# Weight low parts made by an accumulating transfer instead of a VectorE subtraction

## The chip, the cores and the metric

The kernel runs on one core of a Trainium2 chip as a single launch. The time is device microseconds from the first to the last instruction of that core with what the launch adds around it; lower is better. Before the change it is 884.13 us (median of 3 runs, 882.3 to 887.68).

## The reference

Two small transformer stacks stand one behind the other, in fp32, on 256 tokens of width 1024. The first has two layers (a sliding-window attention with sinks, then a block attention), the second two layers that each hold a hybrid mixer (dilated attention beside a state-space model) and a SwiGLU feed-forward of hidden width 2816. Cut to what matters here:

```python
for i in range(2):                                  # first stack
    q, k, v, z = split_proj(rmsnorm(h, norm_g[i]), w_in[i], n_kv)
    h = h + (attention(q, k, v) * silu(z)) @ w_out[i]
for l in range(2):                                  # second stack
    h = h + hybrid_mixer(rmsnorm(h), w_in_2[l], ..., w_out_2[l])
    y = rmsnorm(h)
    h = h + (silu(y @ w_gate[l]) * (y @ w_up[l])) @ w_down[l]
return rmsnorm(h)
```

Nearly all of the arithmetic is `x @ w` with weights that are used once: 141 MB of them are read from memory in each execution. The products have to be close to fp32.

## The kernel before, in words

**Split products.** TensorE multiplies in a rounded fp32 format (`F32R`). Each operand is therefore split into a rounded high part and the low part that is left over, `lo = raw - hi`, and each product is three: hi by hi, hi by lo, lo by hi. For the weights the split is done in `feed`: a raw tile lands from memory (`raw`, up to 8 rows of 128x256), and for each pair of its rows (128x512 elements, 256 KB) a `hi` is cast from it on ScalarE, or on VectorE when VectorE is the earlier one by the planner's reckoning, and a `lo` is made by one VectorE subtraction (line 406). The two are pages of one pool of 64 pages that the activations share.

**Stages.** The stages are named a and ao (first layer and its output product), b and bo, m0, mo0, f0, fo0 (mixer, its output, gate and up products, down product of layer 0), then m1, mo1, f1, fo1. In the profile digits are left out, so `f` is both f0 and f1. A name's stage is the one that was being multiplied when the tile was made, so `f__lo` can hold weights of the down product that follows.

**Order.** A planner writes every engine's program before anything runs. `run_plan` keeps a reckoned clock for each engine (`clk`), issues the weight products of a fixed list slot by slot (one slot is 128 rows of K for 256 output columns), and lets the chains of attention, norms and gates take turns whenever their inputs are reckoned to be ready. `feed` issues casts ahead of the multiplication, `cast_slot` slots against `slot`, as far as pages and the reckoned lead of VectorE and ScalarE allow. Once written, each engine works through its list in order and waits on semaphores: an instruction that waits holds back all that stands behind it on its engine.

**Queues.** All weights are loaded on SyncE's queue in pieces of up to 1 MB into three raw buffers (`RAW = 3`); a load is issued when a buffer's casts are done. GpSimd computes 12 small powers for the norms (`columns`, `final`) and clears 12 small borders (`conv_unit`), and issues no transfers.

Line 78 is the helper that records every operation, so nearly all instructions of the profile stand under L78; the tiles' names tell them apart.

Of the kernel before, what the change touches and what calls it, by code (L numbers as in the profile page):

```python
# [11 lines left out]
F32 = mybir.dt.float32  # L12
F32R = mybir.dt.float32r
BF16 = mybir.dt.bfloat16
I32 = mybir.dt.int32
AF = mybir.ActivationFunctionType
OP = mybir.AluOpType
# [47 lines left out]
class Engine:  # L65


    def __init__(self, build, name, real):
        self.build, self.ename, self.real = build, name, real
# [43 lines left out]
class Build:  # L113
# [33 lines left out]
    SWAP = 100.0  # L147
    WARM = 13
    CAPS_AB = 6
    CAPS = {'mm': 5, 'sc': 3, 'tr': 2, 'pv': 2, 'out': 4}  # L150

    def __init__(self, ctx, tc, io):
        self.tc = tc
        self.nc = Engines(self, tc.nc)
        self.clk = dict(PE=0.0, DVE=0.0, ACT=0.0, POOL=0.0)
        self.cur = Chain(None, 0.0)
        self.cur.start = 0.0
        self.count = 0
        self.io = io
        self.n = 0  # L160
        self.phase = "i"

        def pool(name, bufs, **kw):
            return ctx.enter_context(tc.tile_pool(name=name, bufs=bufs, **kw))

        self.cp = pool("const", 1)
        self.wraw = pool("wraw", self.RAW)
        self.fp = pool("f", self.PAGES)
        self.xp = pool("x", 4)
        self.up = pool("u", 2)  # L170
        self.hp = pool("h", 6)
        self.sp = pool("s", 8)
        psum = dict(space=bass.MemoryType.PSUM)
        self.pp = pool("psum", 8, **psum)
        self.banks = [0.0] * 8
        self.used = dict(mm=0, sc=0, tr=0, pv=0, out=0)
        self.sides = []
        self.ups = self.raws = 0
        self.planned = {}
        self.landing = 0.0  # L180
        self.live = self.wlive = self.most = 0
        self.kept = {}
        self.x = Timed(self)
        self.res = Timed(self)
        self.plan = []
        self.dma_i = self.cast_i = self.cast_k = self.cast_slot = 0
        self.seg_i = self.seg_k = self.seg_m = self.slot = 0
        self.dma_at = 1200.0
        self.queue = self.nc.sync
        self.units = {}  # L190
        self.bubbles = {}


    def name(self, s):
# [89 lines left out]
    def bank_at(self, kind, n=1):  # L284

        if n > 1:
            if self.used[kind] + n > self.CAPS_AB or len(self.banks) < n:
                return None
            return sorted(self.banks)[n - 1]
        if self.used[kind] >= self.CAPS[kind] or not self.banks:  # L290
            return None
# [80 lines left out]
    def feed(self):  # L372

        nc = self.nc
        while self.dma_i < len(self.plan) and self.raws < self.RAW:
            self.feed_dma()
        while self.cast_i < self.dma_i and self.cast_slot < self.slot + self.LEAD:
            now = self.clk["PE"]
            urgent = self.cast_slot < self.slot + self.URGENT
            if not urgent and max(self.clk["DVE"], self.clk["ACT"]) > now + self.AHEAD:  # L380
                return
            s = self.plan[self.cast_i]
            if s["at"] > now:
                self.landing = s["at"]
                return
            k = s["k0"] + self.cast_k
            n = min(2, s["k1"] - k)
            if self.wlive >= self.WMIN and self.wlive + self.live + self.SPARE > self.PAGES:
                return
            self.wlive += 2  # L390
            raw = s["raw"][:, self.cast_k:self.cast_k + n, :]
            hi = self.fp.tile([P, n, S], F32R, tag="f", name=self.name("hi"))
            if s["mode"] == "dt":

                both = hi[:, :, 0:32]
                raw, hi, lo = raw[:, :, 0:16], both[:, :, 0:16], both[:, :, 16:32]
            else:
                lo = self.fp.tile([P, n, S], F32R, tag="f", name=self.name("lo"))
            at = s["at"]
            self.cur = Chain(None, at)  # L400
            self.cur.start = at
            if self.clk["DVE"] + self.SWAP < self.clk["ACT"]:
                nc.vector.tensor_copy(hi, raw)
            else:
                nc.scalar.activation(hi, raw, AF.Copy)
            nc.vector.tensor_sub(lo, raw, hi.bitcast(F32))
            for i in range(n):
                s["parts"][k + i] = ((both if s["mode"] == "dt" else hi)[:, i, :], lo[:, i, :], self.cur.ready)
            self.cast_k += n
            self.cast_slot += n  # L410
            if s["k0"] + self.cast_k == s["k1"]:
                self.cast_i += 1
                self.cast_k = 0
                if s["page"]:
                    self.drop()
                else:
                    self.raws -= 1

    def slot_ready(self):

        s = self.plan[self.seg_i]
        k = s["k0"] + self.seg_k
        if (s["xkey"], k) not in self.x or k not in s.get("parts", ()):
            return None
        t = max(self.x.at[s["xkey"], k], s["parts"][k][2])
        if s["first"] and self.seg_k == 0 and self.seg_m == 0:
            b = self.bank_at("mm", 2 if s["mode"] == "AB" else 1)
            if b is None or (s["mode"] == "half" and len(self.banks) < 2):
                return None
            t = max(t, b, sorted(self.banks)[s["mode"] == "half"])  # L430
        return t
# [1303 lines left out]
```

## Time and profile before

| | us |
|---|---|
| median of 3 runs | 884.13 |
| profiled execution | 884.43 |
| its span, first to last instruction | 882.4 |
| TensorE (PE) busy | 867.1 (98%) |
| VectorE (DVE) busy | 743.5 (84%) |
| ScalarE (ACT) busy | 546.7 (62%) |
| GpSimd (POOL) busy | 13.4 (2%) |
| DMA engines, share of 16 engines' span | 46.7% for 142.30 MB |

The first column of a stage in the profile's tables is its stretch of the span. A matmul's end is modelled and matmuls overlap in the pipeline, so the sum of their durations is more than the busy time; the busy time is their union. A group of instructions reads: engine, operation, out<-in by the tiles' names, partitions x elements, count, then busy time in all, mean ns of one, and the idle time ahead of them with what ended it.

### The profile page before, as it was taken

The page shows a single profiled execution, that of the slowest core. Times are in us where ns is not written, and L with a number is a line of the kernel's source. Part 1 is how long each engine was busy: PE and PEld are TensorE (multiplying, and loading weights), DVE is VectorE, ACT ScalarE, POOL GpSimd, SP SyncE. Part 2 cuts the span into 40 slices and gives each one's busy share as a digit, 9 for nine tenths or more (in the row PEclk, how much of TensorE's full clock was granted, in tenths as well). Part 3 has the DMA queues.
Part 4 walks back from the last instruction along what each step waited for, and adds up shares of the span by engine and source line. Part 5 has one row for each costly group of instructions (what it writes and reads, how often), then busy time and mean ns, then how long its engine had stood idle before and what let it go on. Part 6 is the DMA issues. An engine that isn't in the chain of part 4 may idle for free.

```text
span 882.4 us, 16918 instructions
## 1 busy us (share of the span) xinstructions
PE 867.1 (98%) x6451; PEld 795.9 (90%) x6451; DVE 743.5 (84%) x1677; ACT 546.7 (62%) x1289; POOL 13.4 (2%) x30
## 2 busy tenths in 40 slices
PE   8999999999999999999999999999999999999996
PEld 7987999879998899888888889999999888889996
DVE  5999899998999997999989478988978999888331
ACT  5468764788678775677556355677756676555321
POOL 0000000000100000000000000000000000000000
PEclk9999999999999999999999999999999999999998
DMA  8522675216620047767545537510247576535401
GB/s 301 196 97 73 232 270 173 94 59 220 230 97 13 14 144 233 267 208 269 197 175 167 204 123 289 189 49 2 60 156 263 196 263 209 191 132 190 157 1 48
DMA packets 30385, 142.30 MB, mean 161 GB/s; under 512 B 5344, under 2 KB 6880, under 8 KB 18400
## 3 DMA queue, kind: packets, MB, share of 16 engines
q1 hardware_dynamic: 30016, 141.08, 46.1%
q8 instruction: 51, 0.84, 0.4%
q14 instruction: 30, 0.25, 0.1%
q10 hardware_dynamic: 288, 0.14, 0.1%
HBM read 140.15 MB, written 1.05 MB: 160 GB/s over the span
## 4 chain that ended last, share of the span: by engine, by line
PE 63%; issue 22%; DVE 8%; DMA 4%; ACT 3%; SPq 0%; POOL 0%; POOLq 0%; DVEq 0%; ACTq 0%
PE m__p L78 20%; PE f__p L78 13%; PE b__p L78 8%; PE fo__p L78 7%; PE a__p L78 5%; PE mo__p L78 4%; PE bo__p L78 4%; PE ao__p L78 3%; DVE mo__lo L78 1%; DMA mo__raw<-wg 1%; DMA fo__raw<-wa 1%; DMA cst<-cst 1%; DVE f__lo L78 1%; DVE m__xs L78 1%; DVE m__lo L78 1%
## 5 line engine op out<-in xcount | busy, mean ns | idle before, releaser
L78 PE MATMUL f__p<-mo__x,f__hi 128*128 128x512 f32 x468 | 165.7, 395 | 0.0
L78 PE MATMUL f__p<-mo__x,f__lo 128*128 128x256 f32 x468 | 131.2, 280 | 0.0
L78 DVE TENSOR_TENSOR f__lo<-f__raw,f__hi 128x512 fp32r<-128x512 f32 x172 | 114.6, 688 | 3.8 <-ACT f__hi L78 1.9
L78 PEld LDWEIGHTS f__p<-mo__x,f__hi 128*128 128x128 f32 x468 | 87.7, 187 | 20.6
L78 ACT ACTIVATE f__hi<-f__raw 128x512 fp32r<-128x512 f32 x162 | 92.5, 622 | 0.1
L78 PEld LDWEIGHTS f__p<-mo__x,f__lo 128*128 128x128 f32 x468 | 88.4, 189 | 0.0
L78 PE MATMUL fo__p<-f__r,fo__hi 128*128 128x256 f32 (+1 forms) x300 | 71.3, 320 | 0.0
L78 PE MATMUL f__p<-f__x,f__hi 128*128 128x512 f32 x164 | 59.3, 395 | 0.0
L78 ACT ACTIVATE f__sum<-f__p 128x256 f32<-128x256 f32 x84 | 29.5, 383 | 44.6 <-PE f__p L78 44.6
L78 PE MATMUL fo__p<-f__r,fo__lo 128*128 128x256 f32 x200 | 56.3, 281 | 0.0
L78 PEld LDWEIGHTS fo__p<-f__r,fo__hi 128*128 128x128 f32 x300 | 49.9, 190 | 4.1
L78 PE MATMUL a__p<-fo__x,a__hi 128*128 128x256 f32 x272 | 51.5, 289 | 0.6 <-DVE fo__x L78 0.6
L78 DVE TENSOR_TENSOR fo__lo<-fo__raw,fo__hi 128x512 fp32r<-128x512 f32 (+1 forms) x58 | 36.1, 670 | 14.2 <-ACT fo__hi L78 11.7
L78 PE MATMUL mo__p<-mo__r,mo__hi 128*128 128x256 f32 x256 | 46.8, 284 | 1.1 <-DVE mo__r L78 1.1
L78 DVE TENSOR_TENSOR m__lo<-m__raw,m__hi 128x512 fp32r<-128x512 f32 x61 | 41.2, 686 | 6.9 <-ACT m__hi L78 6.5
L78 PE MATMUL f__p<-f__x,f__lo 128*128 128x256 f32 x164 | 46.0, 280 | 0.0
L78 PEld LDWEIGHTS a__p<-fo__x,a__hi 128*128 128x128 f32 x272 | 42.5, 192 | 2.5 <-issue 1.7
L78 PE MATMUL m__p<-bo__x,m__hi 128*128 128x256 f32 x232 | 44.3, 289 | 0.0
L78 ACT ACTIVATE mo__hi<-mo__raw 128x512 fp32r<-128x512 f32 x48 | 28.5, 626 | 24.3 <-DMA mo__raw<-wo 14.8
L78 DVE TENSOR_TENSOR mo__lo<-mo__raw,mo__hi 128x512 fp32r<-128x512 f32 x50 | 33.1, 688 | 12.3 <-ACT mo__hi L78 12.1
L78 ACT ACTIVATE fo__hi<-fo__raw 128x512 fp32r<-128x512 f32 (+2 forms) x59 | 30.8, 579 | 20.1 <-DMA fo__raw<-w 10.2
L78 PE MATMUL fo__p<-f__r,f__hi 128*128 128x256 f32 (+1 forms) x180 | 42.7, 319 | 0.0
(532 smaller groups left out, 2577.4 us busy)
## 6 DMA issues: line engine op xcount, KB each, us to landing
f__raw<-wu SPq DMA_DIRECT2D x18, 1024.0 KB, 4.9
f__raw<-wg SPq DMA_DIRECT2D x17, 1024.0 KB, 4.8
m__raw<-w SPq DMA_DIRECT2D x13, 1024.0 KB, 5.0
f__raw<-wd SPq DMA_DIRECT2D x10, 1024.0 KB, 4.9
b__raw<-wb SPq DMA_DIRECT2D x6, 1024.0 KB, 4.8
mo__raw<-wo SPq DMA_DIRECT2D x12, 512.0 KB, 4.2
fo__raw<-wd SPq DMA_DIRECT2D x6, 1024.0 KB, 4.9
fo__raw<-w SPq DMA_DIRECT2D x5, 1024.0 KB, 5.6
```

What stands on the lines that cost most here:

```text
L78: return fn(*args, **kw)
```

## The change

For a pair of rows that meets the conditions of `by_dma`, the low part is made in two steps: ScalarE writes the negated high part into `lo` (a copy with scale -1, rounded as `hi` is), and GpSimd issues a transfer that adds the same 256 KB of weights from memory onto it, so that `lo = -hi + raw`. Otherwise the subtraction on VectorE stays. The conditions: a full pair of an ordinary weight tile, cast at least 12 slots ahead of its use, GpSimd's reckoned clock not over 1 us past TensorE's, and ScalarE's reckoned clock earlier than VectorE's. The planner reckons 1300 ns of GpSimd and a further 3500 ns until the transfer has landed.

```diff
+    DMA_POOL = 1300.0
+    DMA_LAND = 3500.0
+    DMA_LEAD = 12
+    DMA_GAP = 0.0
+    NO_DMA = ()
...
-            nc.vector.tensor_sub(lo, raw, hi.bitcast(F32))
+            if self.by_dma(s, n):
+
+                nc.scalar.activation(lo, raw, AF.Copy, scale=-1.0)
+                self.tc.nc.gpsimd.dma_start(out=lo, in_=s["w"][s["unit"], :, k:k + n, :].bitcast(F32R), accum_op=OP.add)
+                self.clk["POOL"] = max(self.clk["POOL"], self.cur.ready) + self.DMA_POOL
+                self.cur.ready = self.clk["POOL"] + self.DMA_LAND
+                self.share[1] += 1
+            else:
+                nc.vector.tensor_sub(lo, raw, hi.bitcast(F32))
+                self.share[0] += 1
...
+    def by_dma(self, s, n):
+
+        return (s["mode"] in ("T", "AB", "tok") and not s["page"] and n == 2 and s["phase"] not in self.NO_DMA
+                and self.cast_slot >= self.slot + self.DMA_LEAD and self.clk["POOL"] < self.clk["PE"] + 1000.0
+                and self.clk["ACT"] + self.DMA_GAP < self.clk["DVE"])
```

Counted over the built programs: 277 low parts of 526 that VectorE subtracted go this way. By the weights they read, 20 belong to b, 52 to m0 and m1, 32 to the output products ao to mo1, 123 to f0 and f1 (60 and 63) and 50 to fo0 and fo1 (28 and 22); a has none. VectorE has 276 tensor_tensor fewer and, since it is now the earlier engine more often, 100 casts of high parts more (34 before, 134 after; 69 of the 100 are f's and fo's). ScalarE has 165 instructions more, which is 277 more less 112 that left it. The number of matmuls is the same, as is the number of transfers on SyncE's queue (196).

GpSimd's queue at the start of f0, where the norm's power stands (`f__s`), before the change:

```order
L78 TENSOR_TENSOR mo__s_4822<-mo__s_4820,mhalf 128x2
L78 TENSOR_TENSOR mo__s_4954<-mo__s_4952,mhalf 128x2
L78 TENSOR_TENSOR f__s_5412<-f__s_5410,mhalf 128x2
L78 TENSOR_TENSOR m__s_7506<-m__s_7504,mhalf 128x2
L78 MEMSET m__u_7589 128x2x3
```

and with it:

```order
L415 DMA f__lo_5469<-wg 128x512
L415 DMA f__lo_5501<-wu 128x512
L415 DMA f__lo_5506<-wu 128x512
L78 TENSOR_TENSOR f__s_5540<-f__s_5538,mhalf 128x2
L415 DMA f__lo_5553<-wg 128x512
L415 DMA f__lo_5578<-wu 128x512
L415 DMA f__lo_5605<-wu 128x512
```

The power that the norm of f0 needs now stands behind the transfers that were issued ahead of it, each of which waits for ScalarE's negated part.

ScalarE in the middle of f0 (`f__sum` reads a finished product, `f__gt` is the gate's tanh, `f__r` the split of the product's input for the next stage), before:

```order
L78 ACTIVATE f__hi_6177<-f__raw_6032 128x512
L78 ACTIVATE f__hi_6192<-f__raw_6077 128x512
L78 ACTIVATE f__r_6196<-f__sum_6143 128x256
L78 ACTIVATE f__r_6197<-f__sum_6143 128x256
L78 ACTIVATE f__sum_6208<-f__p_6137 128x256
L78 ACTIVATE f__sum_6208<-f__p_6138 128x256
L78 ACTIVATE f__hi_6225<-f__raw_6077 128x512
L78 ACTIVATE f__gt_6229<-f__sum_6208 128x512
```

and with the change:

```order
L78 ACTIVATE f__hi_6017<-f__raw_5865 128x512
L78 ACTIVATE f__lo_6018<-f__raw_5865 128x512
L78 ACTIVATE f__r_6027<-f__sum_5993 128x256
L78 ACTIVATE f__r_6028<-f__sum_5993 128x256
L78 ACTIVATE f__hi_6041<-f__raw_5865 128x512
L78 ACTIVATE f__lo_6042<-f__raw_5865 128x512
L78 ACTIVATE f__lo_6051<-f__raw_5865 128x512
L78 ACTIVATE f__sum_6061<-f__p_5987 128x256
L78 ACTIVATE f__sum_6061<-f__p_5988 128x256
```

Between two readings of finished products ScalarE now does up to five weight instructions where it did one or two.

VectorE in the same stage with the change (before, a subtraction `f__lo` stood at nearly every place between the others):

```order
L78 TENSOR_TENSOR f__sum_5807<-f__sum_5807,f__rowh_5594 128x512
L78 SCALAR_TENSOR_TENSOR f__gt_5820<-f__gt_5820,f__sum_5807 128x512
L78 CAST f__hi_5854<-f__raw_5662 128x512
L78 CAST f__hi_5874<-f__raw_5719 128x512
L78 TENSOR_TENSOR f__lo_5875<-f__raw_5719,f__hi_5874 128x512
L78 TENSOR_TENSOR f__sum_5867<-f__p_5799,f__sum_5867 128x256
L78 TENSOR_TENSOR f__sum_5867<-f__p_5800,f__sum_5867 128x256
```

Of the eight subtractions that two units need, about two are left in this stage, and casts have moved in.

## Rows read from the trace of the kernel before

**Rows 1.** The page: busy time and share of the span by engine, instructions.

```profile
PE 867.1 (98%) x6451; PEld 795.9 (90%) x6451; DVE 743.5 (84%) x1677; ACT 546.7 (62%) x1289; POOL 13.4 (2%) x30
```

**Rows 2.** Windows: stretch, length; busy by engine, PEclk, DMA share, GB/s.

```profile
0.00:50.00 50.00, 46.46 (x345) 43.61 (x346) 39.32 (x88) 26.09 (x60) 1.03 (x7) 1.00 0.67 241
50.00:100.00 50.00, 49.22 (x405) 41.93 (x404) 45.87 (x160) 38.25 (x117) 0.00 (x0) 1.00 0.29 99
100.00:850.00 750.00, 746.88 (x5502) 686.25 (x5502) 653.66 (x1422) 478.37 (x1106) 11.72 (x22) 1.00 0.48 166
850.00:882.40 32.40, 24.54 (x205) 24.07 (x203) 4.65 (x9) 4.02 (x8) 0.69 (x1) 0.89 0.10 33
```

**Rows 3.** Windows of 20 us around the idle places of the middle, same columns.

```profile
360.00:380.00 20.00, 19.38 (x113) 16.78 (x112) 19.45 (x39) 13.80 (x31) 0.69 (x1) 1.00 0.64 225
660.00:680.00 20.00, 18.90 (x159) 18.70 (x158) 16.51 (x31) 11.81 (x22) 1.07 (x1) 1.00 0.77 273
680.00:700.00 20.00, 19.01 (x113) 16.33 (x113) 19.46 (x40) 14.23 (x30) 1.07 (x1) 1.00 0.57 203
```

**Rows 4.** The chain that ended last, in f0: start us, us, what.

```profile
361.95 116.45 PE f__p L78 x672
```

**Rows 5.** Groups by form: the weights' splits on DVE and ACT.

```profile
L78 DVE TENSOR_TENSOR f__lo<-f__raw,f__hi 128x512 fp32r<-128x512 f32 x172 | 114.6, 688 | 3.8 <-ACT f__hi L78 1.9 <-DVE f__hi L78 0.5
L78 ACT ACTIVATE f__hi<-f__raw 128x512 fp32r<-128x512 f32 x162 | 92.5, 622 | 0.1
L78 DVE CAST f__hi<-f__raw 128x512 fp32r<-128x512 f32 x10 | 4.2, 422 | 0.0
```

**Rows 6.** Windows of the feed-forward stages: loads to last use, of f0, f0+fo0, f1, f1+fo1.

```profile
341.00:478.00 137.00, 136.38 (x822) 121.39 (x821) 126.49 (x240) 85.97 (x185) 0.69 (x1) 1.00 0.62 215
341.00:539.00 198.00, 197.38 (x1174) 175.18 (x1173) 165.34 (x316) 115.53 (x245) 0.69 (x1) 1.00 0.60 210
663.00:810.00 147.00, 144.91 (x872) 127.66 (x872) 132.42 (x242) 88.52 (x181) 1.07 (x1) 1.00 0.59 207
663.00:858.00 195.00, 192.91 (x1273) 175.66 (x1273) 153.50 (x276) 106.17 (x214) 1.07 (x1) 1.00 0.51 181
```

**Rows 7.** Window in which loads queue up, same columns.

```profile
16.00:22.00 6.00, 5.77 (x47) 5.55 (x47) 4.86 (x12) 4.06 (x12) 0.00 (x0) 1.00 1.01 409
```

**Rows 8.** The page: what the DMA engines moved over the span.

```profile
DMA packets 30385, 142.30 MB, mean 161 GB/s; under 512 B 5344, under 2 KB 6880, under 8 KB 18400
```

**Rows 9.** DMA issues: count, KB each, median us from issue to landing.

```profile
f__raw<-wg SPq DMA_DIRECT2D x17, 1024.0 KB, 4.8
...
mo__raw<-wo SPq DMA_DIRECT2D x8, 256.0 KB, 2.7
```

**Rows 10.** Instructions on one tile: ns min/median/max, first and last start us.

```profile
L1523 SPq DMA_DIRECT2D f__raw<-wg x17: 327/328/328, 357.3 to 754.8; - x17
...
L78 DVE TENSOR_TENSOR fo__lo<-f__raw,fo__hi x20: 683/686/693, 477.5 to 815.7; 128x512 fp32r<-128x512 f32 x20
...
L78 PE MATMUL fo__p<-f__r,fo__lo x200: 279/280/283, 500.7 to 872.0; 128*128 128x256 f32 x100
```

**Rows 11.** GpSimd's groups: the norms' powers.

```profile
L78 POOL TENSOR_TENSOR m__s<-m__s,mhalf 128x2 f32<-128x2 f32 x4 | 4.9, 1223 | 323.6 <-DVE m__s L78 322.8 <-ACT m__dT L78 0.7
L78 POOL TENSOR_TENSOR f__s<-f__s,mhalf 128x2 f32<-128x2 f32 x2 | 1.8, 878 | 64.3 <-DVE f__s L78 64.3
```

More of the change, by code (lines that the diff above doesn't have):

```diff
@@ L191, in __init__ @@
         self.bubbles = {}
+        self.share = [0, 0]
     def name(self, s):
```

## Prediction, before the changed kernel ran

> **What bounds the kernel now.** I read the page's busy shares first, then the busy time by stretch, then the chain of waits, then the DMA shares of the stages that take most transfers.
>
> TensorE is busy for 867.1 of 882.4 us [rows 1]; VectorE, which the change relieves, for 743.5. A high share alone says little, since it is an average, so look at where TensorE is idle [rows 2]: 3.54 us in the first 50 us, 0.78 in the next 50, 7.86 after 850, and 3.12 us in the 750 us between. The start and the end have no transferred low part (a has none, and after 850 only the last products and the final norm are left). So TensorE's idle time that a faster VectorE could remove is those 3.12 us, and 2.7 of them stand in three places, the entries of f0 and f1 and the end of mo1: 0.62, 1.10 and 0.99 us [rows 3]. There the chain runs over VectorE and ScalarE. In the middle of f0 VectorE is at 92% (126.49 of 137 us) [rows 6] and yet the chain is one piece of 116.45 us of TensorE's own matmuls [rows 4]: VectorE is full but never late, and emptying it buys nothing there. The granted clock is 1.00 in all of it [rows 2], which is the upper level, 2.4 GHz.
>
> **The change part by part.**
>
> *VectorE.* A subtraction costs 114.6/172 = 0.666 us, a cast 4.2/10 = 0.42 us [rows 5]. 276 tensor_tensor fewer are -184 us, 100 casts more are +42: busy time falls from 743.5 to about 602 us. This lies beside TensorE's work except at the three places above.
>
> *ScalarE.* A cast of 128x512 costs 92.5/162 = 0.571 us [rows 5], and I take the same for the negated copy. 277 more and 112 fewer are about +94 us: 547 to 641, or 73%. In f0, where 88 of the low parts are cast (60 gate and up, 28 down, some of them after 478), it has 85.97 us of 137 [rows 6]; with all 88 there and no cast given away it would be 86 + 50 = 136 us, and with the 35 casts a layer that VectorE takes over (half of f's and fo's 69), about 116. Fuller than now, and less so than VectorE was without being late. ScalarE reads the finished products, though, so up to five weight instructions (2.9 us) can stand ahead of such a reading; a unit takes TensorE about 5.5 us (116.45 us for 672 matmuls at 32 a unit [rows 4]), and three units' products fit in the banks, so I cost that at nothing. If that cover went, each unit could be late by the 2.9 us.
>
> *GpSimd.* It issues 277 transfers. No row shows it issuing one. From below, SyncE takes 0.33 us to issue [rows 10]; from above I take the dearest thing that GpSimd does here, a norm's power at 1.22 us [rows 11]. In f0 the 60 gate and up transfers would take 20 to 73 us of 137. The powers now stand behind transfers: one that waits is late by one to two issues, 0.3 to 2.4 us. Only the powers at the entries of b, f0, m1 and f1 are followed at once by work that TensorE's next products end in, so the bounds are 0 and 4 x 2.4 = 10 us; I take 1 us, near the lower end, since products that need no row yet run on after the norm starts (TensorE lost just 0.62 us at the entry of f0 [rows 3]).
>
> *Landing.* A plain 256 KB load lands 2.7 us after its issue [rows 9]. A low part has far longer: the first subtraction for the down product starts at 477.5 and the first matmul with such a tile at 500.7 [rows 10], a lead of 23 us. Even three times the plain landing is hidden.
>
> *The DMA engines.* This is the term that decides. 277 x 0.262 MB are 72.6 MB on top of 142.3 [rows 8]. When loads queue up the engines move 409 GB/s at a share of 1.01 [rows 7]; over the stages they move 215 GB/s at 0.62 [rows 6], or 347 GB/s per full share. A plain 256 KB transfer is therefore 0.65 to 0.76 us of all 16 engines. What the addition costs, no row shows. The lower bound is that price; for an upper one I take two to three times it, since the engines must read the tile in SBUF as well as the weights, and write the sum.
>
> In f0 and fo0, from the first load (341) to the last down product (539), the weights themselves are 34.6 MB, 85 us at 409 GB/s or, by the share, 0.60 x 198 = 119 us with the next mixer's first loads in it [rows 6]. The 88 accumulating transfers add 57 to 67 us at the plain price: 142 to 186 of 198 us. So they fit, and the same holds for f1 and fo1 (0.51 x 195 = 99 us, and 85 transfers, 55 to 65 us: 154 to 164 of 195) [rows 6]. At twice the price the first is 199 to 253 of 198 and the second 195 to 229 of 195.
>
> **Sum.** The profiled execution took 884.43 us, 0.30 above the median of the three runs. From it I take 3.1 us of idle time that goes with VectorE's load, add 1 for the powers, and set the rest at nothing because TensorE covers it: 882.3. Matmuls' ends are modelled, so a pause that is shorter than a matmul's tail is not shown as idle; in the same three places some 1 to 2 us of that kind may go too. I forecast **881 us**. The bounds of this case alone: 884.4 - 6 = 878 (twice the shown idle time) and 884.4 + 7 = 891 (the powers late at their upper bound, 10 us, against 3 gained), and a few us lower than 878 if more pauses are hidden than I believe.
>
> **Rivals.**
>
> *The DMA engines become the bound in the feed-forward stages.* For it: f0 and f1 hold 123 of the 277, while 0.6 of the engines' time is already taken there [rows 6]. Against it: the average over the span is 47%, and the low parts have a 23 us lead. It decides from the point where the transfers do not fit: (198 - 119)/88 = 0.90 us of engine time each by the share, (198 - 85)/88 = 1.28 us by the saturated rate [rows 6, 7]. At 1.3 to 1.5 us each the excess is 1 to 55 us in layer 0 and 0 to 34 in layer 1, so the time is 881 plus some 0 to 89; half of it, 30 to 40 us, is not hidden by the lead, and I put this case at 890 to 925, most likely 907. Three times the plain price, 2 to 2.3 us, is 119 + 88 x 2.1 = 304 of 198 and 99 + 178 = 277 of 195, an excess of 188 us and a time near 1040. The sign of it would be TensorE waiting for `lo` or ScalarE for `raw` inside f0, where today it waits for nothing. This is the case on the other side. The Trainium skill, page "Collectives: The Full Stack", section "The bandwidth ceiling: the fold count and why AG ≠ RS ≠ AR", says that an addition in the transfer engines reads two sources through the same read ring, and gives 1.93 for the ratio measured there between plain and adding transfers. By that ratio an accumulating transfer here would be 1.25 to 1.47 us, the case just priced; no run here shows it yet.
>
> *GpSimd becomes the bound.* The 60 transfers of f0 leave 137/60 = 2.3 us each [rows 6]; from there on, low parts are late whatever the engines do. Twice the power's time, 2.4 us, would be just there; at 3 us the excess is 60 x 3 - 137 = 43 us a layer, of which the 23 us of lead take half: about 881 + 40 = 921. Nothing in the trace speaks for an issue that long.
>
> *VectorE's load is worth more than its idle places show.* If the attention stages have hidden pauses throughout, 9 to 12 us could go, 872 to 875. Against it: their idle time is nil, and the matmuls are the same in number and form.
>
> *The change doesn't do what it says* (too few transfers) is excluded by the count: 277 of 526.
>
> **How the numbers follow.** My forecast, no contention felt, has 0.47; the DMA bound at about twice the price 0.30, the dearer kinds of it 0.09, GpSimd's 0.06; VectorE's load worth more than shown 0.08. I call 1%, 8.8 us, the least that can be told from no change. The forecast case lies within 1%, and 0.03 of the DMA case at its mildest: 0.50. Faster by over 1% is the last of these cases, 0.08. Slower is the rest, 0.42. The range reaches from 873, in the middle of the fast case, to 922, which takes in most of the mild DMA case and GpSimd's at its mildest; the dearer ones, 0.09, and the tails of the others stay out. Within the likeliest case alone it is 876 to 890.
>
> **What would show it.** Right: TensorE's chain in f0 still in one piece, VectorE near 600 us, ScalarE near 640, the DMA share in 341 to 539 near 0.9 and not at 1, and no wait of TensorE for a `lo`. Wrong: a median landing of SyncE's 1 MB loads well above 4.8 us [rows 9] with ScalarE idle for `raw` (the DMA engines), or GpSimd busy from end to end with its transfers issued late (GpSimd). If a small 256 KB addition occupies the engines for over 0.9 us, the step that set its price between the plain one and less than 1.4 times it has failed.

## The result, and the profile after

The changed kernel takes **948.56 us** (median of four runs, 945.56 to 955.43), beside 883.21 of the kernel before: a ratio of 1.075, 95% interval 1.0706 to 1.0795. That is slower by 65 us and above the whole range of the prediction. The profiled execution took 945.56 us, its span 943.5. In the ratios below, the kernel before runs on the same chip as the kernel it is compared with (medians from 883.2 to 885.1).

The page of the changed kernel, busy times and the two queues that carry weights (q0 is GpSimd's, q1 SyncE's: packets, MB, share of 16 engines' span):

```profile
PE 883.9 (94%) x6451; PEld 802.4 (85%) x6451; DVE 629.4 (67%) x1505; ACT 635.4 (67%) x1454; POOL 253.5 (27%) x307
...
q0 software_dynamic: 39888, 72.63, 43.0%
q1 hardware_dynamic: 30016, 141.08, 39.9%
```

Against [rows 1], VectorE lost 114 us of work and ScalarE gained 89, as the change intends. TensorE's idle time (span less busy) rose from 15.3 to 59.6 us, and its busy time by 16.8. The last two rows point to the cause, which the experiments below test. The additions move half as many bytes as the loads (72.63 against 141.08 MB) and yet occupy the engines longer: 0.430 x 943.5 us / 277 = **1.465 us** of all 16 engines for one of 256 KB. For the loads the same division gives 0.399 x 943.5 / 141.08 = 2.67 us a MB, 0.70 us for 256 KB.

Stretches of the changed kernel; columns as in [rows 2] (the last three: PEclk, DMA share, GB/s). The last row is the feed-forward of layer 0:

```profile
100.00:150.00 50.00, 46.15 (x372) 44.83 (x372) 34.12 (x64) 37.53 (x72) 19.22 (x22) 1.00 1.05 303
150.00:200.00 50.00, 41.16 (x323) 34.35 (x321) 38.68 (x150) 33.55 (x96) 6.14 (x7) 0.90 0.62 156
...
400.00:450.00 50.00, 50.00 (x290) 44.08 (x289) 34.57 (x70) 40.81 (x89) 18.77 (x22) 1.00 1.07 305
450.00:500.00 50.00, 47.30 (x267) 40.50 (x265) 28.54 (x59) 33.80 (x72) 22.24 (x26) 1.00 1.09 279
500.00:550.00 50.00, 44.22 (x231) 36.83 (x231) 20.55 (x42) 22.17 (x45) 20.14 (x24) 0.93 1.09 279
...
341.00:600.00 259.00, 242.36 (x1464) 214.70 (x1463) 149.45 (x307) 168.49 (x343) 100.60 (x118) 0.97 1.07 292
```

The share is over 1 through all of the feed-forward, where [rows 6] had 0.60 to 0.62, and the engines then move 279 to 308 GB/s instead of the 409 of [rows 7]. (A share over 1 means that packets of the two queues overlap in the records.) TensorE's losses lie in two kinds of places. One is inside the feed-forward (11.5 us idle from 450 to 600 and, in layer 1, 6.9 from 800 to 900). The other is the entries, that is, the starts, of stages: of b (12.7 us from 100 to 200, the largest), of bo and m0 (3.8 from 200 to 250), of f0 (5.1 from 350 to 400) and of f1 (5.2 from 700 to 750). In the 50 us that hold the longest wait, 8.8 us at b, the granted clock is 0.90. Over the span it is 0.982 instead of 0.996, which is about 883.9 x (1 - 0.982/0.996) = 12 us, an estimate, of the 16.8 that TensorE's busy time grew.

The chain of the feed-forward of layer 0 (start us, us, what), the long pieces, and who waits:

```profile
382.42 78.64 PE f__p L78 x446
461.31 18.55 DMA f__lo<-wg
479.90 6.66 PE f__p L78 x37
486.87 16.83 DMA f__lo<-wg
511.33 17.58 DMA f__lo<-wd
```

```profile
PEld fo__p L78 <- DMA f__lo<-wd: 10.2, 9, 2.3
...
PE b__p L78 <- DVE b__rope L78: 8.8, 1, 8.8
PEld f__p L78 <- DMA f__lo<-wg: 8.7, 8, 2.2
```

In [rows 4] this was one piece of TensorE's matmuls. Now it runs so for 78.64 us, in which the lead (the time from a transfer's issue to the first use of what it brings) is used up, and then TensorE waits for low parts. The one that was issued at 461.31 landed 18.55 us later, and TensorE waited 1.5 us for it, so its lead was about 17 us. Landings (count, KB, median us from issue to landing):

```profile
f__raw<-wg SPq DMA_DIRECT2D x14, 1024.0 KB, 8.1
...
f__lo<-wg POOLq DMA_DIRECT2D x51, 256.0 KB, 16.7
...
f__lo<-wd POOLq DMA_DIRECT2D x28, 256.0 KB, 15.6
b__lo<-wb POOLq DMA_DIRECT2D x16, 256.0 KB, 13.3
```

An addition in b and in the feed-forward lands after 13 to 17 us (for the mixers' `m__lo<-w` it is 10.0), and a 1 MB load after 8.1 instead of 4.8 [rows 9].

### The profile page after: what moved, and what is told of

It is laid out like the page before. It is cut to its first block, busy times and chain, and to the rows that moved or that the text cites. A ratio compares the mean times of both kernels' runs of the same rounds, so it can differ in the third digit from the quotient of the medians.

```text
span 943.5 us, 17554 instructions
## 1 busy us (share of the span) xinstructions
PE 883.9 (94%) x6451; PEld 802.4 (85%) x6451; DVE 629.4 (67%) x1505; ACT 635.4 (67%) x1454; POOL 253.5 (27%) x307
## 3 DMA queue, kind: packets, MB, share of 16 engines
q0 software_dynamic: 39888, 72.63, 43.0%
q1 hardware_dynamic: 30016, 141.08, 39.9%
HBM read 212.77 MB, written 1.05 MB: 227 GB/s over the span
## 4 chain that ended last, share of the span: by engine, by line
PE 45%; DMA 28%; ACT 10%; issue 8%; DVE 7%; POOL 1%; SPq 0%; DVEq 0%; POOLq 0%; ACTq 0%
PE f__p L78 17%; PE m__p L78 16%; DMA f__lo<-wg 5%; PE a__p L78 5%; DMA f__lo<-wd 4%; PE b__p L78 4%; PE fo__p L78 3%; DMA fo__raw<-w 2%; DMA mo__raw<-wo 2%; DMA f__lo<-wu 2%; DMA ao__raw<-wb 2%; DMA mo__raw<-wu 2%; DMA bo__raw<-w 2%; DMA m__raw<-wo 1%; DMA mo__lo<-wg 1%
## 5 line engine op out<-in xcount | busy, mean ns | idle before, releaser
L78 PE MATMUL f__p<-mo__x,f__hi 128*128 128x512 f32 x412 | 145.2, 392 | 0.0
L78 ACT ACTIVATE f__lo<-f__raw 128x512 fp32r<-128x512 f32 x120 | 70.9, 618 | 0.0
L78 DVE TENSOR_TENSOR f__sum<-f__p,f__sum 128x256 f32<-128x256 f32 x84 | 32.3, 423 | 55.8 <-ACT f__sum L78 55.8
L415 POOL DMA_DIRECT2D f__lo<-wu x53 | 46.4, 875 | 66.3 <-ACT f__lo L78 22.1
L415 POOL DMA_DIRECT2D f__lo<-wg x51 | 44.7, 876 | 66.7 <-ACT f__lo L78 20.8
L415 POOL DMA_DIRECT2D m__lo<-w x35 | 30.6, 891 | 111.1 <-ACT m__lo L78 88.9
L78 ACT ACTIVATE f__hi<-f__raw 128x512 fp32r<-128x512 f32 x94 | 57.8, 621 | 2.4 <-DMA f__raw<-wu 1.9
L78 PE MATMUL f__p<-mo__x,mo__hi 128*128 128x512 f32 x116 | 43.5, 412 | 3.3 <-DVE mo__x L78 3.3
L78 ACT ACTIVATE fo__hi<-fo__raw 128x512 fp32r<-128x512 f32 (+2 forms) x43 | 23.1, 574 | 29.9 <-DMA fo__raw<-wd 15.3
L78 PE MATMUL fo__p<-f__r,f__lo 128*128 128x256 f32 x120 | 35.7, 297 | 7.6 <-DMA f__lo<-wd 7.5
L78 ACT ACTIVATE m__hi<-m__raw 128x512 fp32r<-128x512 f32 x56 | 35.0, 630 | 10.3 <-DMA m__raw<-wo 7.3
```

The source lines that it names most:

```text
L78: return fn(*args, **kw)
L415: self.tc.nc.gpsimd.dma_start(out=lo, in_=s["w"][s["unit"], :, k:k + n, :].bitcast(F32R), accum_op=OP.add)
```

## The experiments

**Theory:** an addition occupies the transfer engines about twice as long as a plain transfer, so loads and low parts come late. **Rivals:** A, ScalarE's copies and the new order; B, GpSimd (its issues, the powers behind them, the latency of its queue); C, each addition costs a fixed time wherever it is. After run 4 two more: D, all of it comes from the entries of b and the mixers and is carried on as late loads; D', only what saturates a whole stage costs.

**1. The addition turned into a plain transfer.**

```diff
-                self.tc.nc.gpsimd.dma_start(out=lo, in_=..., accum_op=OP.add)
+                self.tc.nc.gpsimd.dma_start(out=lo, in_=...)
```

> The changed kernel with the same 277 transfers of the same bytes on the same queue, which now copy the weights over the low part instead of adding them (so the low parts are the raw weights). Order, ScalarE's negated copies and GpSimd's issues are unchanged. Theory (the price of an addition in the DMA engines, 0.430 x 943.5 / 277 = 1.47 us against 0.70 for plain): the software queue's share falls from 43% to about 20 to 22%, f0 and fo0 then need 119 + 88 x 0.70 = 181 of 198 us, and the time is 878 to 892 us. Rival A (ScalarE's extra copies, or the new order of the instructions): nothing of that changes, 940 to 955 us. Rival B (the landing of GpSimd's transfers, with at most eight of them under way, whatever they do): low parts still land after 10 to 17 us, 930 to 955 us.

Measured 903.22 us, ratio 1.022 (1.0184 to 1.0256). So 45 of the 65 us go with the addition as such: same bytes, same issues, same order. But 19 remain at the plain price, against theory too: 10.3 us of them are idle time of TensorE and 8.7 are longer busy time.

```profile
q0 software_dynamic: 39888, 72.63, 27.4%
...
150.00:200.00 50.00, 46.71 (x380) 39.64 (x380) 42.60 (x161) 37.45 (x108) 3.98 (x8) 0.97 0.34 111
200.00:250.00 50.00, 47.42 (x383) 46.47 (x382) 32.62 (x70) 37.18 (x80) 10.38 (x20) 0.97 0.92 307
...
400.00:450.00 50.00, 50.00 (x291) 44.10 (x290) 33.72 (x70) 39.23 (x84) 15.36 (x29) 1.00 1.03 342
```

A plain transfer on this queue is 0.274 x 901.4 / 277 = 0.89 us, so the addition is 1.6 times it, and 2.1 times the loads' 0.70. The expectation had counted 0.70 and a share of 20 to 22%, where 27.4% came. At 0.89 us the sum for f0 and fo0 is 119 + 88 x 0.89 = 197 of 198 us, so the middle of the feed-forward just fits (no idle time from 400 to 650), as the prediction's sum said. The idle time that is left lies at entries: 8.0 us between 100 and 250, 3.3 between 300 and 400, 1.7 between 650 and 750.

**2. An eighth of the bytes.**

```diff
-                self.tc.nc.gpsimd.dma_start(out=lo, in_=s["w"][s["unit"], :, k:k + n, :]..., accum_op=OP.add)
+                self.tc.nc.gpsimd.dma_start(out=lo[0:16], in_=s["w"][s["unit"], 0:16, k:k + n, :]..., accum_op=OP.add)
```

> The changed kernel with the same 277 adding transfers, each on 16 of the 128 partitions only (an eighth of the bytes; the other partitions' low parts stay the negated high part). Order, ScalarE's copies, the number of GpSimd's issues and waits are unchanged. Theory (engine time): about 5% of the engines' span goes to the additions, 878 to 890 us. Rival A (ScalarE's copies, the order): 940 to 955 us. Rival B (GpSimd: its issue time, the powers behind transfers, the latency of its queue): 920 to 955 us, since none of these goes with the bytes.

Measured 882.2 us, ratio 0.9991 (0.9966 to 1.0017). Rivals A and B are out: all of ScalarE's copies, the order and 277 issues on GpSimd are there.

```profile
PE 867.0 (98%) x6451; PEld 798.0 (90%) x6451; DVE 628.1 (71%) x1505; ACT 634.1 (72%) x1454; POOL 225.3 (26%) x307
...
100.00:150.00 50.00, 47.39 (x383) 47.21 (x382) 39.80 (x78) 41.88 (x81) 18.88 (x25) 0.97 0.84 271
```

On the same page VectorE is 115 us emptier and the time is the same. Idle time went at the entry of f0 (0.62 us, [rows 3]) and 2.61 us of it appeared at the entry of b, so even an eighth of the bytes is felt there. The gain and this loss were not taken apart.

**3. The additions alone, in the order of before.**

```diff
             nc.vector.tensor_sub(lo, raw, hi.bitcast(F32))
+            if ... n == 2 and self.cast_slot >= self.slot + 12:   (in the change's proportions by stage)
+                self.tc.nc.gpsimd.dma_start(out=lo, in_=s["w"][s["unit"], :, k:k + n, :].bitcast(F32R), accum_op=OP.add)
```

> The kernel before, in its own order and with all VectorE subtractions kept; 265 of the low parts, in about the proportions of the change (mo0 has one), get an adding transfer of their weights behind the subtraction (so these low parts hold the weights once too often). No copy on ScalarE is added and no instruction of another engine moves. Theory (engine time, 265 x 1.47 = 390 us more of the 16 engines): nearly the whole loss is there without the change's copies and order, 930 to 965 us, with a DMA share of 1 or more in f0, f1 and b. Rival A (ScalarE's copies, the order): 882 to 892 us. Rival B (GpSimd's queue): a loss as in the theory, but with the DMA share below 1.

Measured 958.02 us, ratio 1.0852 (1.0817 to 1.0887): the whole loss and 9 us more, with no copy added and nothing moved. Its chain in f0 and its queue:

```profile
q0 software_dynamic: 38160, 69.49, 40.4%
```

```profile
406.38 19.16 DMA f__lo<-wu
...
433.64 22.31 DMA f__lo<-wu
```

0.404 x 956.2 / 265 = 1.46 us each, the same price again.

**4. One addition in 5 us.** The condition `self.clk["PE"] >= self.next_dma`, set 5000 ns ahead with each addition, leaves 103.

> The changed kernel with one more condition: at least 5 us of TensorE's reckoned clock between two adding transfers, which leaves 103 of the 277 (the planner's order follows). Theory (a threshold: what counts is whether loads and additions fit in the engines): f0 and fo0 need 119 + 40 x 1.47 = 178 of 198 us, so the loss is gone but for a few us at the entries of b, where loads are late at once: 880 to 892 us. Rival C (each addition costs, wherever it is: 61 us / 277 = 0.22 us): 883 + 103 x 0.22 = 906 us. Rival A (ScalarE's copies): likewise in proportion, near 906 us.

Measured 901.88 us, ratio 1.0197 (1.0169 to 1.0225): a miss, near rival C's 906. But the loss is not spread as C has it. The feed-forward from 400 to 550 has no idle time, while 100 to 250 has 11.1 us of it. Runs 5 and 6 take the places apart.

**5 and 6. Only the feed-forward; everything but the feed-forward.**

```diff
-    NO_DMA = ()
+    NO_DMA = ("ao", "b", "bo", "m0", "mo0", "m1", "mo1")     (5)
+    NO_DMA = ("f0", "f1", "fo0", "fo1")                      (6)
```

> The change in the weights of gate, up and down alone (164 of the 277 transfers, at full density; attention and mixer as before). The reading after the first four runs: two losses that add up. In the feed-forward stages the engines are over-full (f0 and fo0: 119 + 84 x 1.47 = 242 of 198 us), which in the changed kernel left TensorE 31 us idle between 350 and 600 and between 700 and 900; this part alone gives 883 + 25 to 35 = 908 to 918 us. Rival C (each addition costs the same 0.22 us wherever it is): 883 + 36 = 919 us. Rival D (the loss comes from the entries of b and of the mixers, and is carried into the feed-forward stages as late loads): 885 to 900 us.

> The change everywhere but in the weights of gate, up and down (105 of the 277 transfers: 20 of b, 8 of bo, 53 of m0 and m1, 23 of mo0 and mo1, 1 of ao). Two losses that add up: the entries of b, bo and m0 lost 16 us in the changed kernel and the entries of f0 and f1, where loads run behind mo's additions, up to 10: 900 to 912 us, with the DMA share below 1 in f0 and f1 and TensorE not idle there. Rival C (0.22 us for each): 883 + 23 = 906 us, spread over all stages that have additions, m0 and m1 too. Rival D' (only saturation over a whole stage costs): 883 to 890 us.

Measured 920.82 us, 1.0396 (1.0362 to 1.0429), and 926.02 us, 1.046 (1.0418 to 1.0501). Both parts cost more than expected (918 and 912 us at most), and together 77 us, over the 65 of the whole, so they don't simply add up. Run 5 alone lies near C's 919, but 164 additions cost 36 us and 105 cost 41, where C had 906 us for run 6, so C's fixed price is out. Run 5 loses without an addition at b, which takes D out. In run 6 TensorE has no idle time from 400 to 550 and from 750 to 850, while f0's entry still loses 5.1 us (350 to 400); and between 100 and 250 the share is 1.05, 0.62 and 0.86 in turn, not full as a whole, and TensorE idles 17.5 us there; that speaks against D'.

```profile
150.00:200.00 50.00, 41.26 (x326) 34.41 (x324) 38.45 (x150) 33.61 (x97) 6.04 (x7) 0.90 0.62 156
...
400.00:450.00 50.00, 50.00 (x284) 43.35 (x284) 47.74 (x91) 32.51 (x73) 0.00 (x0) 1.00 0.65 230
```

**7. A planner that knows the price.** It books 1500 ns of the engines for each addition and allows one only when its reckoned loads have landed; 57 are left.

```diff
+                self.dma_at = max(self.dma_at, self.clk["PE"]) + 1500.0
...
+                and self.dma_at <= self.clk["PE"])
```

> The changed kernel whose planner counts an addition as 1.5 us of the transfer engines and allows one only when its reckoned loads have all landed: 57 are left. Theory (additions cost only where they delay loads): 880 to 886 us. Rival C (0.22 us for each): 883 + 13 = 896 us. That it beats the kernel before: its planner reckons 1.7 us less, and TensorE's idle time that a faster VectorE could remove was 3.1 us, so at most 880.

Measured 893.46 us, ratio 1.008 (1.0048 to 1.0112): a miss by 7 us. In its profiled execution (888.53 us) TensorE's idle time stands between 150 and 250 (4.1 us, before 0.3) and 350 and 400 (2.5, before 0.6), again behind b's entry and at f0's. So the condition doesn't tell the places where an addition is free. One reading, which was not tested, is that a load issued a little later still meets the addition.

**8. Only inside the feed-forward, 5 us apart.** Run 5's list, run 4's spacing, and `self.phase[0] == "f"`: 55 additions.

> Additions only for weights of gate, up and down, only while these stages are already being multiplied, and at least 5 us of TensorE's reckoned clock apart: 55. Theory (there the loads need 0.6 of the engines, and 119 + 29 x 1.47 = 162 of 198 us fit): 882 to 886 us, TensorE without idle time from 400 to 550 and from 700 to 850. Rival C (0.22 us for each): 883 + 12 = 895 us.

Measured 884.72 us, ratio 1.0002 (0.9979 to 1.0026): as expected, and against C's 895.

**9. Only the weights of b:** 20 additions, `NO_DMA` with all other stages.

> Additions for the weights of b alone (20 of the 277). Reading so far: at the entry of b the loads have no slack, whatever the average share is, and each addition in the way makes a load late: most of the 17 us that TensorE idled there with all additions, and the lower granted clock after it, come back: 892 to 902 us. Rival C (0.22 us for each, wherever): 883 + 4 = 887 us. Rival D' (only saturation over a whole stage): 883 to 886 us, since 20 x 1.47 = 29 us in a stage of 90 us whose loads take about half of the engines' time.

Measured 902.89 us, ratio 1.0221 (1.0173 to 1.0269), 0.9 us above the range expected and 0.93 us for each of 20 additions. Its stretches, its landings, and what ScalarE and TensorE wait for between 100 and 200:

```profile
100.00:150.00 50.00, 46.13 (x377) 45.14 (x376) 35.14 (x65) 37.17 (x72) 18.51 (x21) 1.00 1.04 307
150.00:200.00 50.00, 43.56 (x354) 37.02 (x353) 42.39 (x159) 32.27 (x96) 0.00 (x0) 0.93 0.37 107
```

```profile
b__raw<-wb SPq DMA_DIRECT2D x5, 1024.0 KB, 9.0
...
b__lo<-wb POOLq DMA_DIRECT2D x16, 256.0 KB, 15.0
```

```profile
ACT b__hi L78 <- DMA b__raw<-wo: 6.7, 4, 3.0
PE b__p L78 <- DVE b__rope L78: 6.4, 1, 6.4
ACT b__hi L78 <- DMA b__raw<-wb: 5.7, 4, 2.1
PE b__p L78 <- DMA b__lo<-wb: 2.0, 3, 1.1
```

Half of a stage at 1.04 is enough. In the chain of this stretch a 9.07 us piece is the small table of positions, whose landing was 3.7 us before: it sits on SyncE's queue behind the late loads, and the rotation of b's queries and keys (`b__rope`) waits for it. TensorE's one wait for that rotation is 6.4 us of the 10.3 that it idles in this stretch. How much of the loss this table alone costs was not tried. A warning stood in the trace of before, in ScalarE's waits, while TensorE was idle there for 0.04 us in 100. The stretches of before, and those waits:

```profile
100.00:150.00 50.00, 50.00 (x419) 49.98 (x419) 48.88 (x93) 31.58 (x60) 1.01 (x1) 1.00 0.69 241
150.00:200.00 50.00, 49.96 (x418) 42.34 (x417) 47.00 (x167) 36.34 (x105) 0.00 (x0) 1.00 0.26 86
```

```profile
ACT b__hi L78 <- DMA b__raw<-wb: 4.8, 4, 2.0
ACT b__hi L78 <- DMA b__raw<-wo: 3.5, 2, 2.3
```

Six times a cast there had waited for its load already, 8.3 us in all, where f's casts on ScalarE had 0.1 us of idle time in front of them [rows 5]. The average share (0.69 and 0.26 in b's two halves) didn't show it. This reading was made after the loss was known.

**10. The dose in the feed-forward.** Run 8 at 2 us instead of 5: 108 additions, 57 in f0 and fo0.

> As the run with 55 additions in the gate, up and down weights, but at 2 us apart instead of 5: 108 of them, 57 in f0 and fo0. Theory (a sum that has to fit): 119 + 57 x 1.47 = 203 of 198 us, just at the edge: TensorE idles little or not at all in the middle of f0, 883 to 895 us, against 921 with 84 in these stages. Rival C (0.22 us for each): 883 + 24 = 907 us.

Measured 885.69 us, ratio 1.0022 (1.0001 to 1.0044): 108 additions nearly for nothing, with the sum at the edge, against 36 us for 164.

```profile
450.00:500.00 50.00, 50.00 (x290) 44.09 (x289) 32.99 (x65) 32.73 (x67) 16.74 (x19) 1.00 1.05 274
```

```profile
371.54 105.44 PE f__p L78 x607
476.98 61.01 PE fo__p L78 x352
```

The share is over 1 here too, and TensorE's chain runs in these two pieces from 371 to 538. Casts wait for their loads as well:

```profile
ACT f__hi L78 <- DMA f__raw<-wg: 7.1, 6, 4.3
...
ACT f__hi L78 <- DMA f__raw<-wu: 4.7, 5, 1.9
```

A full share is therefore no loss by itself, and neither is a cast that waits. The reading that fits is that the queued work is still done within the lead: low parts land after 8.0 to 11.1 us here, after 13 to 17 in the changed kernel.

**11. Only inside m0 and m1:** 38 additions.

> Additions only while the mixers m0 and m1 themselves are being multiplied, for their own and their output's weights no further than that stage (38, 18 and 20; by the condition the output's weights are left out): in the stretch 250 to 330 loads take 0.1 to 0.5 of the engines. Theory: no loss from the middle of the mixer, a few us where m0's and m1's entries still load: 882 to 888 us. Rival C: 883 + 8 = 891 us. If it is over 895, a low share over a stretch does not show the slack of its loads.

Measured 889.26 us, ratio 1.0061 (1.0032 to 1.0091), 1 us above the range expected and 2 below rival C's 891, so it doesn't tell the two apart. Idle time between 200 and 300 is 2.71 us, where before it was 0.37.

**12. The price by itself.** Groups of transfers, each waiting for the one before.

> Transfers alone, nothing else at work (the computation is left out, and the output is zeros): by turns, each group waiting for the one before, one and eight plain 256 KB loads on SyncE's queue, one and eight on GpSimd's, one and eight additions of 256 KB, then three plain loads and three additions of 1 MB. If the price of an addition is the engines' own: a 2048-byte packet of an addition takes about 176 ns here too, against 84 for a plain one on SyncE's queue and about 98 on GpSimd's, eight additions take about 8 x 1.47 = 12 us and eight plain loads about 6, and a single addition lands in 4 to 5.5 us. If it is contention with the loads: alone an addition's packet is near the plain one's and eight of them take about 6 to 7 us. For the 1 MB additions: 5.5 to 6 us each if the price goes by bytes (an 8192-byte packet in about 620 to 700 ns against 309), less if it goes by packets.

One execution; windows inside two groups (the last two numbers are DMA share and GB/s): first three plain 1 MB loads on SyncE's queue, then three 1 MB additions.

```profile
56.00:60.00 4.00, 3.30 (x3) 0.00 (x0) 1.00 1.02 428
...
68.00:78.00 10.00, 0.31 (x2) 0.00 (x0) 1.00 1.03 215
```

```profile
sp_large<-wd SPq DMA_DIRECT2D x3, 1024.0 KB, 7.0
add_large<-wd POOLq DMA_DIRECT2D x3, 1024.0 KB, 12.2
sp_small<-wu SPq DMA_DIRECT2D x8, 256.0 KB, 4.9
q_small<-wu POOLq DMA_DIRECT2D x8, 256.0 KB, 5.1
add_small<-wu POOLq DMA_DIRECT2D x8, 256.0 KB, 8.4
...
sp_one<-wg SPq DMA_DIRECT2D x1, 256.0 KB, 3.0
q_one<-wg POOLq DMA_DIRECT2D x1, 256.0 KB, 3.3
add_one<-wg POOLq DMA_DIRECT2D x1, 256.0 KB, 4.0
```

Alone, too, the engines move additions at 215 GB/s and plain loads at 428: a factor of 1.99 that needs no contention. The trace's packet records say the same: medians of 629 ns for 8192 bytes of an addition against 309 for a plain load, and of 178 against 84 for 2048 bytes. So it goes by bytes, and larger pieces don't cure it. GpSimd's queue as such is not the reason: its plain transfers went in packets of 4096 bytes here, with a median of 159 ns, as on SyncE's queue in the kernel before. For 256 KB an addition has 8 packets of 2048 bytes on each of the 16 engines, 8 x 178 ns = 1.42 us, near the 1.465 of the changed kernel. A single addition lands in 4.0 us, only 0.7 later than a plain transfer on the same queue, and eight at once in 8.4. In the changed kernel up to eight were under way at once (for 209 us of the span, from issue to landing), beside the loads, so most of the 13 to 17 us there is queueing. The Trainium skill, page "Collectives: The Full Stack", section "The bandwidth ceiling: the fold count and why AG ≠ RS ≠ AR", gives 1.93 for the ratio of plain to adding transfers between ranks; here about the same shows, 1.99 to 2.1, for an addition from memory onto a tile.

| additions | where | loss against before, us | each |
|---|---|---|---|
| 277 | everywhere | 65.4 | 0.24 |
| 20 | b | 18.6 | 0.93 |
| 105 | all but feed-forward | 40.9 | 0.39 |
| 103 | everywhere, 5 us apart | 17.9 | 0.17 |
| 57 | where no reckoned load is under way | 8.4 | 0.15 |
| 164 | feed-forward, full density | 35.7 | 0.22 |
| 38 | inside m0, m1 | 5.0 | 0.13 |
| 108 | inside the feed-forward, 2 us apart | 1.4 | 0.01 |
| 55 | inside the feed-forward, 5 us apart | -0.4 | 0 |

Losses are differences of medians. No version was faster than the kernel before. The best, runs 2, 8 and 10, equal it within 0.3%.

## Why the prediction was wrong

**The step that failed is the price of an addition in the DMA engines.** The forecast set it between the plain price (0.65 to 0.76 us) and 1.4 times that, beside an outer bound of two to three times, and named 0.9 us as the point from which this step has failed: it is 1.465 us in the changed kernel, 1.46 in run 3, and twice the plain price alone in run 12. The rival "the DMA engines become the bound", at 1.3 to 1.5 us, was therefore the case that happened, with its signs: TensorE waiting for `lo`, loads at 8.1 us. The forecast put the plain price first although the ratio of 1.93 and the thought that the tile must be read as well both stood beside it; that no row showed the price was taken as a reason for the lower bound.

**A second step failed with it, and the rival had it wrong too: the sum over whole stages.** The prediction asked only whether transfers fit in 198 us of f0 and fo0, and costed all other stages at nothing. At the plain price that sum came out right in the feed-forward, yet run 1 lost 19 us, with its idle time at the entries; and 20 additions in b alone cost 18.6 us. That is why even the mild case, 890 to 925, was too low: it had the feed-forward's share of the loss (36 us in run 5, where it said 30 to 40) and none of b's, bo's and the mixers'. A stage's average share does not show the lead of its loads; the waits of the casts for `raw` in the trace of before set b apart from f, though such waits alone cost nothing in run 10.

**The landing.** The 23 us of lead [rows 10] were counted for the low part's own transfer, at three times 2.7 us. Queued behind others it took 13 to 17 us, and the same engines delayed the raw loads, for which no lead was worked out. The 23 us also belong to one kind of tile in the kernel before. The condition of the change asks for 12 slots only, which is about 8.3 us of TensorE's time (an estimate: 116.45 us for 672 matmuls, four a slot [rows 4]), and less than the landing that came.

**What held.** VectorE's load was worth next to nothing, as the prediction had it: with it 115 us emptier and an eighth of the additions' bytes the time is the same (run 2). The 3.1 us of idle time that it hoped to gain show in no run's time; in run 2 some of it went and 2.61 us appeared at b. ScalarE came to 635.4 us (641 forecast), and its five weight instructions in a row cost nothing that run 2 shows. The powers behind the transfers made TensorE wait 3.0 us (2.3 at mo, 0.7 at b), where 1 us was taken. GpSimd's issue is 0.86 us (f__lo<-wg, median 862 ns), within the 0.33 to 1.22 bounds, and no bound (run 2). VectorE came to 629.4 us instead of 602. The rows' durations are unchanged (a subtraction 688 ns before, 692 after), but busy time is a union: VectorE's durations add up to 857 us before, in 743.5 of busy time, because each starts under the tail of the last; with fewer in a row less of that overlap is left (711 in 629.4).

**Still open:** why the parts of runs 5 and 6 cost 77 us apart and 65 together; how much of b's loss is the late table of positions; and how much of TensorE's longer busy time is the clock. None of these was tried by itself.

## What to carry to other kernels

- An addition in the transfer engines cost two transfers here. Price it so before moving work there, and where no row shows the price, forecast with the dearer end if a mechanism is at hand.
- Fit transfers into the lead of the loads they share engines with, place by place, not into a stage's average. Look first at places where casts already wait for their loads: 20 transfers at one of them cost more than 108 in stages whose own weights had hardly such waits before (0.3 and 1.5 us). It is a sign and no proof, since in run 10 casts waited and nothing was lost.
- An engine at 84% that hardly anybody waited for was worth nothing to relieve here, and the engine it is relieved by may have a queue that somebody does wait for.

## What the runs showed of the hardware

- Additions from memory onto a tile in SBUF: 215 GB/s with the engines full, plain loads 428. The Trainium skill, page "DMA: Bandwidth & Descriptors", section "Specifications", names a fabric ceiling of 435 GB/s; the 428 lies just under it.
- Plain 256 KB transfers from GpSimd's queue cost 0.89 us of the engines (run 1), loads from SyncE's, most of them in larger pieces, 0.70 (changed kernel).
- The DMA engines at a share of 1.05 are harmless in run 10 (450 to 500), and run 5, with 1.03 to 1.09 from 350 to 550, loses 36 us.
- The 8.8 us wait of TensorE in the changed kernel (160 to 169) ends at the lower level of the clock, 1.2 GHz: the granted clock was 1.00 from 160 to 165, 0.50 from 165 to 175 and 0.97 from 175 to 180. The same three matmuls that started every 0.36 us before the wait started every 0.64 us behind it. In run 8, without such waits, the feed-forward from 350 to 600 shows 1.00 throughout.

```profile
170.00:175.00 5.00, 5.00 (x24) 4.23 (x22) 4.12 (x15) 3.51 (x11) 0.54 (x1) 0.50 0.97 265
```
